# A hybrid pooling and SSD decoder layer: D times x moved from ScalarE into VectorE's sum, and the opening and the w_o pieces of the chunk stage reordered

## The chip, the core and the metric

The kernel runs on one core of one Trainium2 chip. A core has five engines with an instruction stream each: TensorE (PE in the profile; PEld is its loading of weights), VectorE (DVE), ScalarE (ACT), GpSimd (POOL) and SyncE (SP), which here only issues transfers. ACT issues transfers too, so each of the two has a queue of them. An engine takes its instructions in the order of its stream and stands still while the first one waits for a semaphore. SBUF holds tiles of 128 partitions, PSUM takes the results of matmuls in eight banks.

The metric is the time of one execution on the device in microseconds; less is better. The time before is 1295.18 us, the median of three runs (1295.17 to 1296.12).

## The reference

One layer of a decoder, for a prompt of 1024 positions and 8 samples of 8 positions, 1088 columns in all. A pooling branch and a state-space (SSD) branch run side by side and are merged by gates:

```python
shift, scale, gate = jnp.split(jax.nn.silu(c) @ w_ada + b_ada, 3, axis=-1)
h = rmsnorm(x, norm_g) * (1 + scale[:, None]) + shift[:, None]
u_pool, z_pool, z_ssm, xbc, dt_raw, g_raw = jnp.split(h @ w_in, SPLITS, axis=-1)
p, pool_new = pool_mix(u_pool, pool_buf, pos0, pool_w, pool_scale)
p = (p * jax.nn.silu(z_pool)) @ w_pool_out
xbc_c, conv_new = causal_conv(xbc, conv_buf, conv_w, conv_b)
...
y, ssm_new = ssd(xs, dt, A, Bm, Cm, ssm_state)
y = (y + d_skip[:, None] * xs).reshape(b, L, D_INNER)
y = rmsnorm(y * jax.nn.silu(z_ssm), ssm_norm_g)
s = y @ w_ssm_out
m = sigmoid(g_raw)[..., :D_MODEL] * p + sigmoid(g_raw)[..., D_MODEL:] * s
x = x + gate[:, None] * (m @ w_o)
```

The SSD goes over the prompt in chunks of 128 positions. Within one, with a lower triangular decay:

```python
decay = jnp.exp(jnp.where(mask, acs[:, :, None] - acs[:, None, :], -jnp.inf))
att = jnp.einsum('bign,bjgn->bijg', Cq, Bq)[..., None] * decay * dq[:, None]
y = jnp.einsum('bijge,bjgep->bigep', att, xq)
y = y + jnp.einsum('bign,bige,bgepn->bigep', Cq, jnp.exp(acs), h)
h = h * jnp.exp(last)[..., None, None] + jnp.einsum('bjgn,bjge,bjgep->bgepn', Bq, w_in, xq)
```

`d_skip` is the D of the title: after the SSD, D times x is added to y, a factor per head. All is in float32; the large products are made of three matmuls each on values split into a rounded high part and a low rest.

## The kernel before

**Order of the work.** The kernel is one straight program. The order in which instructions are written is not the order in which they are issued: a scheduler goes over the whole program with a model of the chip and places each instruction when the model says that its inputs and buffers are ready, so work may be issued long before its written place. Three things hold it. `in_line(engines)` chains the instructions that were written in a stretch, on the engines named, in their written order (PE through the whole chunk stage). `behind(engine)` keeps what a block writes on that engine behind the last instruction that had been written on it. And tiles have a number of buffers: a new tile of a tag waits until the oldest buffer's last reader has finished, and a pool that is opened where another was closed waits for what used that memory.

**The stages.** From 0 to about 818 us: the conditioning, h, the input projection, the convolution, the pooling, and the samples' SSD. The finished pieces go to scratch in DRAM: `xbc_d` (x, B and C after the convolution), `z_d`, `acs_d` (summed decays), `gp_d`, `gs_d` (gates). From about 818 to 1117 us the chunk stage, which the change edits. After it come the last products of w_ssm_out, the output products with w_o, and the final norm.

**The chunk stage** has 32 chunks, 4 groups g of 8 heads by 8 chunks c (i = 8g + c), and beside them the products of P (pooling) and S (SSD output), in pieces of one block of 352 or 384 columns, 12 matmuls each. `products(t)` draws about 2.56 pieces a chunk. P's pieces end in a product on DVE (line 1721), the S pieces of the first group in a copy on ACT (line 1739), those of later groups in a sum on DVE (line 1742); either frees one of the three PSUM buffers `mm`. The four buffers `ps` serve the chunks.

A chunk is a generator (`chunk`, line 1488) with these steps:

1. Loads of `xb` (line 1491; x, B and C of the chunk, 384 KB, three buffers) and `dec` (line 1187, in `decays`, 512 KB, three buffers), both on SP.
2. ACT makes `cE` (line 1498, but for c = 0); POOL masks `dec` (`far`, line 1192); ACT turns it into 8 exponentials (`exps`, line 1201).
3. The row: load of `sz`; PE turns x, 4 transposes (line 1506), and B (1508), and multiplies B by C (1509) into `pbc`; ACT copies `bt` (1511) and C (1513); DVE makes `xd` (1517), `xw` (1519, one buffer) and multiplies `dec` (1520) and `cE` (1522) by parts of `pbc`. ACT makes `xD`, D times x, in four copies with a scale (line 1525).
4. PE multiplies the new state (1530) and the output `pi` (`inner`, 1213 and 1216). The state is carried on (1534 on ACT, or 1536 on POOL and 1538 on DVE). DVE adds `pi` and `xD` (line 1542). `finish` multiplies by z on DVE (1468), squares on ACT (1469), adds squares on POOL (1470 to 1476), and splits into high `yh` on ACT (1478) and low `yl` on POOL (1479).
5. For c = 7 the last state is transposed and stored through a tile of the tag `xD` (lines 1549 to 1551).

The loop (line 1798) interleaves them: chunk i+1's row, P and S pieces, chunk i's step 4, chunk i+3's loads, chunk i+2's step 2, more pieces. Ahead of it, step 1 and 2 of chunk 0 are written into the stage before (`samples_beside`), and four pieces of P before chunk 0's row.

**The w_o pieces** (`wo_splits`, line 1766): w_o is read in 16 pieces of 128 x 512, each rounded on ACT into `ph` (line 1777, one buffer), stored from ACT (1778), subtracted on POOL (1779) and the rest stored from SP (1773). The raw pieces `pw` have two buffers. The loop calls it twice a chunk from the 14th on.

**The states' update of the samples** (line 1329) is not touched: four times on DVE, `h0` times a per-partition factor plus PSUM, 128 columns each.

## Time and profile before

| | |
|---|---|
| median of the runs | 1295.18 us |
| the profiled execution's own time | 1297.28 us |
| its span | 1295.4 us |
| its mean granted TensorE clock | 0.996 |
| PE busy in its span | 1258.9 us |
| bytes moved | 251.68 MB |

The span runs from the first to the last instruction of the profiled execution. Durations in the profile come from that one execution; times in it are counted from the span's start. A group's row reads: line, engine, operation, tile written <- tiles read, shapes, count | busy time, mean ns of one | idle time of the engine just before them and what ended it. A row of waits reads: who <- whom, us in total, times, the longest. A row of a timeline reads: start, duration, engine, line, operation, tiles, count, and in brackets the idle time before it and what ended that. A row of one line's instructions gives the least, median and greatest duration in ns and the first and last start. DMAs in a timeline stand where they are issued; PEq, ACTq, SPq are the sequencers.

### The profile page before, as it was taken

Reading aid. Unit: us, or ns where it says so; the run is one execution under the profiler, and the core shown is the slowest. Engines: PE = TensorE matmul, PEld = TensorE weight load, DVE = VectorE, ACT = ScalarE, POOL = GpSimd, SP = SyncE. Lnnn points to the kernel's source line nnn. Section 1 sums busy time; section 2 is a strip of 40 time slices with the busy share of each in tenths; the row PEclk is TensorE's granted clock in tenths of the full one; section 3 lists DMA queues with packets and bytes.
Section 4 is the critical chain, followed back from the end, with each engine's and each line's share of the span. In section 5 each row is a group of like instructions: output and inputs, shape, how many; then the busy total and the mean of one; then the engine's idle time right before and its main releaser. Section 6 shows DMA issues by size and latency. Waiting matters only on the chain.

```text
span 1295.4 us, 26382 instructions
## 1 busy us (share of the span) xinstructions
PE 1258.9 (97%) x9739; PEld 1170.7 (90%) x9739; DVE 893.3 (69%) x1512; ACT 699.5 (54%) x1658; POOL 671.9 (52%) x563
## 2 busy tenths in 40 slices
PE   7999999999999999999999999999998999999998
PEld 6779999989999999999999999888897889999786
DVE  4686678966979688676766675577665877476433
ACT  4665347365656555555666543687886776201111
POOL 1007668677868777564445444266675656214000
PEclk9999999999999999999999999999999999999999
DMA  9736355465456544444566574999887665475631
GB/s 330 242 115 223 113 163 164 147 203 177 136 161 212 157 144 149 151 146 135 169 182 192 154 207 159 336 362 382 296 270 249 200 210 171 160 262 161 227 105 50
DMA packets 233793, 251.68 MB, mean 194 GB/s; under 512 B 31265, under 2 KB 177905, under 8 KB 233658
## 3 DMA queue, kind: packets, MB, share of 16 engines
q1 hardware_dynamic: 161568, 171.60, 41.6%
q10 hardware_dynamic: 72098, 78.41, 17.6%
q8 instruction: 77, 1.26, 0.4%
q14 instruction: 50, 0.41, 0.1%
HBM read 167.06 MB, written 83.01 MB: 193 GB/s over the span
## 4 chain that ended last, share of the span: by engine, by line
PE 73%; issue 8%; DMA 6%; POOL 4%; ACT 4%; DVE 4%; ACTq 0%; SPq 0%; POOLq 0%; DVEq 0%
PE mm L608 7%; PE ps L608 7%; PE ps L609 7%; PE ps L610 7%; PE mm L610 6%; PE mm L609 6%; PE mm L359 4%; PE mm L360 4%; PE mm L361 4%; PE ps L1213 2%; PE ps L1997 2%; PE ps L1995 2%; PE ps L1996 2%; PE pc L1530 2%; PE ps L1216 2%
## 5 line engine op out<-in xcount | busy, mean ns | idle before, releaser
L168 POOL TENSOR_TENSOR wlo<-rawA,whi 128x512 fp32r<-128x512 f32 x120 | 180.0, 1505 | 176.8 <-ACT whi L165 100.3
L168 POOL TENSOR_TENSOR wlo<-raw,whi 128x512 fp32r<-128x512 f32 x92 | 147.2, 1607 | 123.2 <-ACT whi L165 109.3
L359 PE MATMUL mm<-Y,whi 128*128 128x352 f32 (+1 forms) x480 | 164.2, 342 | 2.0 <-ACT G L1739 1.4
L360 PE MATMUL mm<-Y,whi 128*128 128x352 f32 (+1 forms) x480 | 158.1, 329 | 1.0 <-DVE Y L1566 1.0
L361 PE MATMUL mm<-Y,wlo 128*128 128x352 f32 (+1 forms) x480 | 157.5, 328 | 0.0
L608 PE MATMUL mm<-Y,whi 128*128 128x272 f32 x496 | 146.5, 295 | 0.7 <-DVE GA L624 0.5
L610 PE MATMUL mm<-Y,wlo 128*128 128x272 f32 x496 | 144.2, 291 | 2.9 <-POOL wlo L168 2.4
L608 PE MATMUL ps<-Y,whi 128*128 128x272 f32 x496 | 143.4, 289 | 2.3 <-ACT o L808 2.2
L609 PE MATMUL ps<-Y,whi 128*128 128x272 f32 x496 | 143.0, 288 | 0.0
L609 PE MATMUL mm<-Y,whi 128*128 128x272 f32 x496 | 142.6, 288 | 0.0
L610 PE MATMUL ps<-Y,wlo 128*128 128x272 f32 x496 | 142.6, 287 | 0.0
L1056 DVE SCALAR_TENSOR_TENSOR GA<-GA,cvT,GA 128x1112 f32<-128x1112 f32 x72 | 128.5, 1787 | 1.6 <-ACT GA L1053 1.5
L165 ACT ACTIVATE whi<-rawA 128x512 fp32r<-128x512 f32 x125 | 78.3, 627 | 88.8 <-PE ps L609 44.9
L165 ACT ACTIVATE whi<-raw 128x512 fp32r<-128x512 f32 x96 | 58.9, 627 | 105.7 <-DVE raw L554 51.3
L359 PEld LDWEIGHTS mm<-Y,whi 128*128 128x128 f32 x480 | 90.8, 189 | 8.8 <-issue 4.6
L610 PEld LDWEIGHTS mm<-Y,wlo 128*128 128x128 f32 x496 | 93.4, 188 | 4.7 <-POOL wlo L168 3.5
L608 PEld LDWEIGHTS mm<-Y,whi 128*128 128x128 f32 x496 | 93.3, 188 | 3.4 <-ACT whi L165 0.7
L608 PEld LDWEIGHTS ps<-Y,whi 128*128 128x128 f32 x496 | 93.3, 188 | 2.9 <-ACT o L808 2.4
L609 PEld LDWEIGHTS mm<-Y,whi 128*128 128x128 f32 x496 | 93.4, 188 | 0.9
L610 PEld LDWEIGHTS ps<-Y,wlo 128*128 128x128 f32 x496 | 93.4, 188 | 0.0
L609 PEld LDWEIGHTS ps<-Y,whi 128*128 128x128 f32 x496 | 93.3, 188 | 0.0
L360 PEld LDWEIGHTS mm<-Y,whi 128*128 128x128 f32 x480 | 90.8, 189 | 1.7 <-DVE Y L1566 1.6
(450 smaller groups left out, 3801.1 us busy)
## 6 DMA issues: line engine op xcount, KB each, us to landing
rawA<-in_w_in SPq DMA_DIRECT2D x46, 512.0 KB
dec<-acs_d SPq DMA_DIRECT2D x32, 512.0 KB
xbc<-GA ACTq DMA_DIRECT2D x24, 512.0 KB
xb<-xbc SPq DMA_DIRECT2D x32, 384.0 KB
rawA<-in_w_in SPq DMA_DIRECT2D x32, 256.0 KB
pw<-in_w_ssm_out ACTq DMA_DIRECT2D x32, 256.0 KB
ws<-ph ACTq DMA_DIRECT2D x32, 256.0 KB
ws<-pw SPq DMA_DIRECT2D x32, 256.0 KB
```

The costliest lines, as they stand in the source:

```text
L165: ins = act(hi[:, :, :ncols], raw[:, :, :ncols], AF.Copy)
L168: (eng or nc.gpsimd).tensor_tensor(lo[:, :, :ncols], raw[:, :, :ncols], hi[:, :, :ncols].bitcast(F32), ALU.subtract)
L359: mm(ps[:, :n], a, rh[k][:, o:o + n], start=(k == 0), stop=False)
L360: mm(ps[:, :n], a, rl[k][:, o:o + n], start=False, stop=False)
L361: mm(ps[:, :n], b, rh[k][:, o:o + n], start=False, stop=(k == nk - 1))
L608: mm(p, hi, ah, start=(k == 0), stop=False)
L609: mm(p, hi, al, start=False, stop=False)
L610: mm(p, lo, ah, start=False, stop=(k == 3))
L1056: V.scalar_tensor_tensor(d[:, :n], rp[:, k:k + n], cvT[:, 24 * k + mc:24 * k + mc + 1], d[:, :n], ALU.mult, ALU.add)
L1213: mm(o[hh], xd[:S, 2 * q + hh, :], dec[:S, 2 * q + hh], start=True, stop=state is None)
L1216: mm(o[hh], state[:, h * 64:h * 64 + 64], cE[:, h], start=False, stop=True)
L1530: mm(pu, bt, xw.rearrange("p h d -> p (h d)"), start=True, stop=True)
```

## The change

D times x is no longer copied by ScalarE: the sum of `pi` and `xD` becomes four `scalar_tensor_tensor` on VectorE, each 128 columns of x times the factor plus `pi`. The tag `xD` goes; the last states get a tile `fo` of their own, one buffer in the pool `ck`. In `finish` the copy to `yh` and the subtraction to `yl` come ahead of the squares. For the first chunk the row is written ahead of `far` and `exps`, and ahead of all pieces of P; `far` and `exps` of the first chunk leave the stage before; the opening's instructions are chained on PE, ACT and DVE instead of on PE, and the `behind` blocks of the first chunks go. In `wo_splits` a piece is rounded one step later than before, its rest is stored in the step after, and what the calls in the loop write is kept behind ACT, SP and POOL.

```diff
-    CKL = ("sz", "xD", "v")
+    CKL = ("sz", "v")
...
         V.tensor_tensor(v, v, sz, ALU.mult)
+        yhc = yh[g][:, :, o:o + S]
+        act(yhc, v, AF.Copy)
         act(sz, v, AF.Square)
+        nc.gpsimd.tensor_tensor(yl[g][:, :, o:o + S], v, yhc.bitcast(F32), ALU.subtract)
         nc.gpsimd.tensor_tensor(sz[:, 0:2], sz[:, 0:2], sz[:, 2:4], ALU.add)
...
-        yhc = yh[g][:, :, o:o + S]
-        act(yhc, v, AF.Copy)
-        nc.gpsimd.tensor_tensor(yl[g][:, :, o:o + S], v, yhc.bitcast(F32), ALU.subtract)
...
-        far(dec, c)
-        exps(dec, g, c)
-        yield
+        if g > 0 or c > 0:
+            far(dec, c)
+            exps(dec, g, c)
+            yield
         sz = ckt([P, 4, P], "sz", 3)
...
+        if g == c == 0:
+            yield
+            far(dec, c)
+            exps(dec, g, c)
         V.tensor_tensor(dec, dec, pbc[:, P:2 * P].unsqueeze(1).to_broadcast([P, 8, P]), ALU.mult)
...
-        xD = ckt([P, 4, P], "xD")
-        for q in range(4):
-            act(xD[:, q], xb[:, q], AF.Copy, scale=Dv[:, 4 * g + q:4 * g + q + 1])
...
-        V.tensor_tensor(v, pi, xD, ALU.add)
+        for q in range(4):
+            V.scalar_tensor_tensor(v[:, q], xb[:, q], Dv[:, 4 * g + q:4 * g + q + 1], pi[:, q], ALU.mult, ALU.add)
         finish(g, o, P, v, sz)
...
-            fo = ckt([P, 4, P], "xD")
+            fo = ckt([P, 4, P], "fo", 1)
...
-        if due[0] == 7 * LAST - 1:
-            with behind(mybir.EngineType.Activation):
-                next(seq[0])
...
-            if n > 1:
-                load(wo_d[(n - 2) // 2][:, 1, n % 2 * 512:n % 2 * 512 + 512], raws.pop(n - 2))
             yield
-            if n < 16:
+            if 0 < n < 17:
                 hi = ck.tile([P, 512], F32R, tag="ph", name=nm("ph"), bufs=1)
-                act(hi, raws[n], AF.Copy)
...
+                act(hi, raws[n - 1], AF.Copy)
...
+                lo = raws.pop(n - 1)
             yield
+            if 0 < n < 17:
+                load(wo_d[(n - 1) // 2][:, 1, (n - 1) % 2 * 512:(n - 1) % 2 * 512 + 512], lo)
...
-    in_line((mybir.EngineType.PE,), True)
-    with behind(mybir.EngineType.Activation):
-        next(seq[1])
-    for _ in range(FRONT):
+    first_engines = (mybir.EngineType.PE, mybir.EngineType.Activation, mybir.EngineType.DVE)
+    in_line(first_engines, True)
+    next(seq[0])
+    for _ in range(FRONT - 1):
         next(pc_)
     next(seq[0])
+    next(seq[1])
+    next(pc_)
+    in_line(first_engines)
     for i in range(len(seq)):
         if i > 12:
-            next(wos, None)
+            with behind(mybir.EngineType.Activation), behind(mybir.EngineType.SP), behind(mybir.EngineType.Pool):
+                next(wos, None)
         if i + 1 < len(seq):
-            with behind(mybir.EngineType.DVE, 1 - i) if i < 2 else ExitStack():
-                next(seq[i + 1])
+            next(seq[i + 1])
         products(i + 0.4)
...
         if i + 2 < len(seq):
-            with behind(mybir.EngineType.Activation) if i == 0 else ExitStack():
-                next(seq[i + 2])
+            next(seq[i + 2])
         products(i + 1.0)
```

The second call of `wo_splits` in the loop gets the same three `behind`.

More of the change, by code (lines that the diff above doesn't have):

```diff
@@ L1771, in wo_splits @@
                 load(raws[n], w_o[0, n // 2 * P:n // 2 * P + P, n % 2 * 512:n % 2 * 512 + 512])
-            if n > 1:
-                load(wo_d[(n - 2) // 2][:, 1, n % 2 * 512:n % 2 * 512 + 512], raws.pop(n - 2))
             yield
-            if n < 16:
+            if 0 < n < 17:
                 hi = ck.tile([P, 512], F32R, tag="ph", name=nm("ph"), bufs=1)
-                act(hi, raws[n], AF.Copy)
-                store_(wo_d[n // 2][:, 0, n % 2 * 512:n % 2 * 512 + 512], hi.bitcast(F32))
-                nc.gpsimd.tensor_tensor(raws[n].bitcast(F32R), raws[n], hi.bitcast(F32), ALU.subtract)
+                act(hi, raws[n - 1], AF.Copy)
+                store_(wo_d[(n - 1) // 2][:, 0, (n - 1) % 2 * 512:(n - 1) % 2 * 512 + 512], hi.bitcast(F32))
+                nc.gpsimd.tensor_tensor(raws[n - 1].bitcast(F32R), raws[n - 1], hi.bitcast(F32), ALU.subtract)
+                lo = raws.pop(n - 1)
             yield
+            if 0 < n < 17:
+                load(wo_d[(n - 1) // 2][:, 1, (n - 1) % 2 * 512:(n - 1) % 2 * 512 + 512], lo)
     wos = wo_splits()
@@ L1807, in tile_pool_ssd_step @@
         if i > 12:
-            next(wos, None)
+            with behind(mybir.EngineType.Activation), behind(mybir.EngineType.SP), behind(mybir.EngineType.Pool):
+                next(wos, None)
         next(seq[i], None)
```

## The prediction

> **What bounds the kernel now.** First the page's busy shares and its chain of waits, by engine.

> ```profile
> PE 1258.9 (97%) x9739; PEld 1170.7 (90%) x9739; DVE 893.3 (69%) x1512; ACT 699.5 (54%) x1658; POOL 671.9 (52%) x563
> PE 73%; issue 8%; DMA 6%; POOL 4%; ACT 4%; DVE 4%; ACTq 0%; SPq 0%; POOLq 0%; DVEq 0%
> ```

> TensorE sets the time, and the change leaves its matmuls as they are. What can be won is the time in which PE stands still, so I next read what PE waited for from 806 us, just ahead of the chunks, to 1104 us, and the busy time by stretch.

> ```profile
> PE ps L1506 <- DVE cE L1522: 2.1, 1, 2.1
> PE ps L1508 <- DVE cE L1522: 1.7, 1, 1.7
> PE mm L359 <- ACT G L1739: 1.4, 1, 1.4
> PE pc L1530 <- ACT bt L1511: 1.3, 1, 1.3
> PE mm L360 <- DVE Y L1566: 1.0, 1, 1.0
> PE ps L1213 <- DVE dec L1520: 0.4, 1, 0.4
> ```

> ```profile
> 842.00:971.00 129.00, 129.00 (x1052) 114.61 (x1051) 92.48 (x119) 105.73 (x293) 90.11 (x99) 1.00 0.97 327
> 971.00:1004.00 33.00, 27.81 (x212) 24.18 (x211) 17.62 (x25) 20.89 (x58) 18.53 (x21) 1.00 0.78 251
> 1004.00:1104.00 100.00, 100.00 (x819) 88.52 (x817) 78.48 (x114) 73.45 (x208) 61.15 (x77) 1.00 0.61 188
> ```

> Six waits, 7.9 us, are all of it; apart from them PE is busy 100% of the chunk stage (the columns are stretch, its length, then PE, PEld, DVE, ACT, POOL busy). The table is a little short: a matmul's record runs some 0.15 us into the next one's.

> ```profile
> 818.85 0.33 PE L361 MATMUL mm<-Y,wlo 128*128 128x384 f32 x1
> 819.02 0.34 PE L359 MATMUL mm<-Y,whi 128*128 128x384 f32 x1
> 820.40 0.45 PE L360 MATMUL mm<-Y,whi 128*128 128x384 f32 x1 [1.04 <-DVE Y L1566]
> ```

> From start to start these are 0.17 apart, then 1.38: the wait is worth 1.21, not 1.04. With 0.14 more for each of the six, PE loses 7.9 + 0.8 = 8.7 us. That is the ceiling of the gain.

> Three of the waits, 2.7 listed (3.1 from start to start), lie at the opening; three, 5.2 listed (5.6), between 977 and 1003 us. Their causes on ACT and DVE:

> ```profile
> 833.29 0.69 DVE L1519 TENSOR_TENSOR xw<-ps,wdT 128x512 f32<-128x512 f32 x1 [3.91 <-DMA gs<-u]
> 834.49 0.25 ACT L1511 ACTIVATE bt<-ps 128x128 f32<-128x128 f32 x1
> ```

> ```profile
> 975.61 0.63 ACT L1777 ACTIVATE ph<-pw 128x512 fp32r<-128x512 f32 x1 [2.96 <-DMA pw<-in_w_o]
> 978.37 0.44 ACT L1739 ACTIVATE G<-mm 128x352 f32<-128x352 f32 x1
> 984.49 0.33 ACTq L1778 DMA_DIRECT2D wo<-ph  x1
> 991.97 0.63 ACT L1777 ACTIVATE ph<-pw 128x512 fp32r<-128x512 f32 x1 [4.82 <-DMA wo<-ph]
> 993.00 1.28 ACT L1525 ACTIVATE xD<-xb,Dv 128x128 f32<-128x128 f32 x4 [0.40 <-DMA out<-xD]
> ```

> ```profile
> 970.96 0.33 SPq L1771 DMA_DIRECT2D pw<-in_w_o  x1
> ```

> The second group is the w_o pieces' doing. ACT runs in order; at 972.65 it came to the rounding of a piece whose load had been issued at 970.96, and stood 2.96 us. Everything behind it was late: the copy L1739 that frees a PSUM buffer, and by way of L1513 the two products of DVE that free `pbc`. PE lost 1.4 + 2.1. At 987.15 ACT stood 4.82 us more for the store of the one `ph` buffer; PE lost 1.7 at 1001.

> **The change part by part.**

> *D times x.* Removed from ACT: 4 copies a chunk, and their waits; added on DVE: 4 products-and-sums of 128 columns in place of one sum of 512.

> ```profile
> L1525 ACT ACTIVATE xD<-xb,Dv 128x128 f32<-128x128 f32 x120 | 38.8, 390 | 22.1 <-DVE v L1542 17.4 <-DVE xd L1517 3.3 <-DMA out<-xD 1.4
> L1542 DVE TENSOR_TENSOR v<-ps,xD 128x512 f32<-128x512 f32 x29 | 19.9, 686 | 3.9 <-PE ps L1216 3.5 <-PE ps L1213 0.4
> 780.77 2.16 DVE L1329 SCALAR_TENSOR_TENSOR h<-h,E,ps 128x128 f32<-128x128 f32 x8 [1.38 <-PE ps L1326]
> ```

> ACT gains 38.8/120 x 4 = 1.29 us a chunk and up to 22.1 us of standing in all. The new form stands in the trace: the states' update L1329, SBUF times a per-partition scalar plus PSUM, 8 in 2.16 us, 0.27 each. Four cost 1.08 against 0.69: DVE +0.39 a chunk, 12.5 us over 32 chunks. On the path it costs nothing while DVE has room: it is busy 78.5 of the 100 us from 1004 on, so some 83 after (11.5 chunks). Without that cover it would be 12.5 us.

> Whether 0.27 holds beside a busy POOL is the open price.

> ```profile
> L1468 DVE TENSOR_TENSOR v<-v,sz x36: 425/750/1828, 841.4 to 1113.7; 128x512 f32<-128x512 f32 x32, 128x256 f32<-128x256 f32 x4
> ```

> L1468, two inputs in SBUF, runs from its least to 2.4 times its median (750 to 1828 ns); L1542, one of two in PSUM, hardly varies. Bounds 0.27 and 0.27 x 1828/750 = 0.66 for one, so +0.39 to +1.95 a chunk; I take 0.27, the same form. At the upper end DVE would be at 78.5 + 1.95 x 11.5 = 101 of 100, the bound. [...]

> *xb is held longer.* `xb` was last read by the ACT copies, early in a chunk; now the sum reads it, last. Its three buffers turn, so the load for chunk i+3 waits on SP for chunk i's sum, with all SP has behind it (decays, z, weights), and PE's transposes of chunk i+3 wait for the load.

> ```profile
> 1059.00 0.52 SPq L1491 DMA_DIRECT2D xb<-xbc  x1
> 1069.09 0.35 SPq L1187 DMA_DIRECT2D dec<-acs_d  x1
> 1076.04 0.32 SPq L459 DMA_DIRECT2D whi<-ws  x1
> ```

> ```profile
> 1070.88 0.68 DVE L1542 TENSOR_TENSOR v<-ps,xD 128x512 f32<-128x512 f32 x1
> 1081.06 0.60 PE L1506 MATMUL ps<-ident,xb 128*128 128x128 f32 x4
> ```

> The 30th load goes out at 1059.00, 22 us ahead of its transposes at 1081.06. After the change it can't go before the sum at 1070.88 has ended, at 1072.0 with 0.39 more: 9.1 us ahead. How long does a load of 384 KB take? The w_o piece above, 256 KB, took from 970.96 to 975.6, 4.6 us; by size that gives 6.9, so 4.6 to 6.9, and 2.2 to 4.5 us are left. I cost it at nothing. Without that room: behind the weight load that SP held until 1076.04 it goes out at 1076.4 and lands at 1081.0 to 1083.3, so PE waits 0 to 2.3 us.

> *Opening.* The 7 transposes and products of chunk 0 go ahead of the pooling products, which stood at 819 for DVE.

> ```profile
> 827.98 0.60 PE L1506 MATMUL ps<-ident,xb 128*128 128x128 f32 x4
> 828.75 0.60 PE L1506 MATMUL ps<-ident,xb 128*128 128x128 f32 x4
> ```

> They take 828.75 - 827.98 = 0.77 us and fill that much of the 1.21. `bt` (ACT, 834.49), `xw`, `xd` and the decay product move some 8 us ahead of PE's need, so the waits of 1.3 and 0.4 (2.0 from start to start) go. Sum 2.7. What can spoil it: ACT and DVE are now kept in written order, and `xw`, which waited until 833.29 for a store of the stage before, stands ahead of the sums that free the pooling products' PSUM (a rival below). The decays' mask and 8 exponentials of chunk 0 leave the stage before, where PE has no wait on them.

> *w_o pieces.* A piece is rounded one step later, about a chunk after its load was issued: a chunk is (1081.06 - 827.98)/29 = 8.7 us, the load 4.6. The store of `ph` took 984.49 to 991.97, 7.5 us, and the next rounding now comes 8.7 us on. Both ACT waits go, and with them the 5.6.

> ```profile
> L1771 SPq DMA_DIRECT2D pw<-in_w_o x16: 332/486/2146, 830.7 to 981.9; - x16
> L1864 SPq DMA_DIRECT2D Y<-wo x7: 320/422/517, 1135.1 to 1202.1; - x7
> SPq L1771 <- DMA wo<-pw: 12.4, 6, 5.7
> ```

> The trace has the pieces 120 us ahead of their written place (they are written into the loop from the 14th chunk on and start at 830.7, beside the 1st). Kept behind SP, ACT and POOL they now start near 950, where the DMA share is soon 0.61 instead of 0.97, and end near 1100, 35 us before the first load of the finished w_o at 1135.1. On SP a piece's load still waits for the store of the piece two before it, up to 5.7 us, with the chunk's loads behind it. It did so before without PE waiting for a chunk's load; I cost it at nothing, and let it count for the last rival. The subtractions on POOL have its idle time, 39 of 100 us from 1004 on.

> *Copy ahead of square; own buffer for last states.* Same instructions on ACT and POOL, in another order; the own buffer drops the 0.40 at 993. Both hidden by PE's 100%.

> *Sum.* 2.7 + 5.6 = 8.3 off. For new short waits I allow 0.6 (the least of the six, 0.4 + 0.14, is nearest), with bounds 0 and 2.1, the largest. Net 7.7: the span of 1295.40 becomes 1287.7. The profiled execution's own time, 1297.28, is 1.9 above its span and 2.1 above the median of 1295.18; the saving is the same for each, so the median becomes 1287.5. Own range: 1286.4 (all 8.7) to 1289.8.

> **Rivals.**

> *The pieces go on hurting.* If the wait at 975.6 comes back at another chunk, 3.8 us (1.4 + 2.1 + 0.3) stay: 1291.3. For: one `ph` buffer, two `pw`, a 7.5 us store against 8.7. Against: ACT has 1.29 us a chunk more.

> *The opening is spoilt.* If `xw` still waits until 833.3, the pooling sums behind it on DVE start near 834, and PE, which has three PSUM buffers for them and comes to the fourth block near 826 (four were done by 827.98), stands about 8 us; the cluster's gain is used up: 1295. For: 3.91 <- DMA gs<-u. Against: the buffers lie elsewhere, since one is added, and that ACT may store sooner; no row shows it.

> *xb comes late: slower.* The load sits behind another wait of SP's at half the 29 chunks that reload, 1.15 us (the middle of 0 to 2.3) each: 14.5 x 1.15 = 17 lost, 8 won, 1304. It decides from 0.38 us a chunk (11 us over 29), where the time passes 1297.8. For:

> ```profile
> SPq L459 <- PE mm L361: 29.8, 12, 6.7
> ```

> SP stands 2.5 us on average in 12 such waits, 6.7 at most. Against: the decays, three buffers too, are loaded behind the same chunk's matmuls already, and PE waits for none. DVE as the bound is the same sign, and needs the upper price.

> **How the numbers follow.** Forecast 60%, pieces 12%, opening 10%, `xb` 18%. A measurement of this kernel can't tell less than about 0.2% (2.6 us) from no change: faster means under 1292.6, so 72%; within 10%; slower 18%. The range runs from below the ceiling's 1286.4 up to 1296.5, past the spoilt opening, and leaves the slower case out.

> **What would show it.** Right: PE's waits from 806 to 1104 sum to 1 us or less; the pooling products' wait is near 0.4; no ACT wait of over 1 us on L1777's line; the four sums take 1.1 us together; the transposes never wait for `xb`. Wrong: PE's transposes (L1506) wait for DMA xb or SP's L1491 stands for DVE longer than 4 us; DVE over 95% busy in the chunks; PE standing near 826 for the pooling sums.

## The result, and the profile after

The changed kernel takes 1299.75 us (median of 19 runs, 1296.54 to 1302.65); the kernel before took 1295.17 us in as many runs on the same chips. The ratio is 1.0030, 95% interval 1.0018 to 1.0042: slower by 0.3%, about 4.6 us. The forecast was 1287.5, its range ran from just under 1286.4 to 1296.5; both missed, on the slower side. The profiled execution took 1301.79 us, its span 1300.1, at a mean granted TensorE clock of 0.992 (0.996 before).

First the page's busy shares, then the view of TensorE's waits over the same stretch as before, 806 to 1104 us (total us, times, longest).

```profile
PE 1263.0 (97%) x9739; PEld 1173.4 (90%) x9739; DVE 901.5 (69%) x1608; ACT 662.4 (51%) x1528; POOL 668.3 (51%) x563
```

```profile
PE ps L1507 <- DMA xb<-xbc: 6.7, 5, 2.2
PE ps L1509 <- DVE cE L1527: 1.8, 1, 1.8
PE ps L1216 <- POOL sq_acc L1479: 0.4, 1, 0.4
PE mm L360 <- DVE Y L1569: 0.3, 1, 0.3
```

The six waits of before are gone, all but 0.3 us of the opening's, as forecast. In their place stand five waits for xb and one for VectorE's `cE`: 9.2 us listed where 7.9 were. (Lines have moved: x is turned at 1507, B at 1509, the products that free `pbc` stand at 1525 and 1527, the four sums at 1545, the w_o pieces at 1771 to 1781.)

Part of the loss is not in that table. The view by stretch, here in steps of 3.41 us, has the granted clock in the third column from the end.

```profile
869.86:873.27 3.41, 1.17 (x8) 0.91 (x7) 0.89 (x2) 0.76 (x3) 0.27 (x1) 1.00 0.93 283
873.27:876.69 3.42, 1.61 (x8) 1.24 (x9) 3.19 (x4) 1.89 (x5) 2.61 (x5) 0.50 0.54 177
876.69:880.10 3.41, 3.41 (x13) 3.41 (x13) 3.03 (x8) 2.79 (x9) 1.29 (x2) 0.50 0.93 294
880.10:883.51 3.41, 3.41 (x39) 2.48 (x38) 2.82 (x4) 0.76 (x3) 2.06 (x3) 1.00 0.83 225
...
1101.96:1105.38 3.42, 3.42 (x14) 3.42 (x13) 3.42 (x8) 1.45 (x3) 2.79 (x3) 0.50 0.88 240
```

PE waits at 870.6, and from 873.27 on it runs at half speed for 6.83 us: "busy" for the whole of 876.69 to 880.10, but with its matmuls of 352 columns 0.29 us from start to start, where they are 0.16 apart at full clock. (The 39 of the next stretch are mostly shorter ones.) The same follows the wait of 1099.5, for 3.42 us. In the chunk stage the kernel before shows no half clock at all. 10.25 us at half speed are up to 5.1 us lost. That holds for the profiled execution, whose clock, 0.992, is among the lowest of the nineteen. Their mean is 0.9942, and 0.9956 in the 122 executions of the kernel before that were timed beside the experiments; the difference of 0.0014 comes to 1.8 us an execution.

What made PE stand at 870 is seen on VectorE and on SyncE's queue (start, us, instruction, idle before it and what ended it).

```profile
863.95 0.68 DVE L1518 TENSOR_TENSOR xd<-ps,dtT 128x512 f32<-128x512 f32 x1
872.05 0.43 DVE L1468 TENSOR_TENSOR v<-v,sz 128x256 f32<-128x256 f32 x1 [7.42 <-DMA v<-ys]
...
873.50 1.22 DVE L1525 TENSOR_TENSOR dec<-dec,ps 128x1024 f32<-128x1024 f32 x1 [0.56 <-ACT ps L1514]
874.64 1.21 DVE L1527 TENSOR_TENSOR cE<-cE,ps 128x1024 f32<-128x1024 f32 x1
```

```profile
863.59 0.53 SPq L1485 DMA_DIRECT2D v<-ys  x1
864.21 0.58 SPq L1491 DMA_DIRECT2D xb<-xbc  x1
```

```profile
870.62 0.32 PE L361 MATMUL mm<-Y,wlo 128*128 128x352 f32 x1
873.18 1.02 PE L1507 MATMUL ps<-ident,xb 128*128 128x128 f32 x4 [2.24 <-DMA xb<-xbc]
876.00 0.45 PE L1509 MATMUL ps<-ident,xb 128*128 128x128 f32 x1 [1.81 <-DVE cE L1527]
```

Once in each group, behind the fourth chunk, the samples' rows are finished too (`sample_end`: loads of their gate and of `ys_d`, and line 1468 on 64 columns of each quarter). In the changed kernel their product is issued on VectorE ahead of the next chunk's `dec` and `cE` products; its operand was asked for at 863.59 and is there at 872.0, so VectorE stands 7.42 us with everything behind it. In the kernel before the same product stood behind those two and, in this group, waited for nothing:

```profile
872.62 1.22 DVE L1522 TENSOR_TENSOR cE<-cE,ps 128x1024 f32<-128x1024 f32 x1
873.75 0.94 DVE L1468 TENSOR_TENSOR v<-v,sz 128x256 f32<-128x256 f32 x1
```

The change leaves that product and its loads as written. The scheduler, which places each instruction by its own model, drew a new order.

Start to start, PE's waits over 0.25 us in the chunk stage sum to 11.87 us against 8.74: +3.1. With up to 5.1 at half clock, of which some 1.7 is in those waits already, that is 6.5; by the records of PE, from the last matmul of line 610 to the first that adds up the squares, the stage took 323.0 us against 316.6, +6.4. The stages ahead of it took 1.4 less, those after it 0.3 less. With the clock's mean share, 1.8, in place of this execution's, waits and clock come near the 4.6 of the medians; the waits, 3.1, are those of one execution each.

### The profile page after: what moved, and what is told of

Same layout as the page of the kernel before. It is cut to its first block, busy times and chain, and to the rows that moved or that the text cites. A ratio compares the mean times of both kernels' runs of the same rounds, so it can differ in the third digit from the quotient of the medians.

```text
span 1300.1 us, 26323 instructions
## 1 busy us (share of the span) xinstructions
PE 1263.0 (97%) x9739; PEld 1173.4 (90%) x9739; DVE 901.5 (69%) x1608; ACT 662.4 (51%) x1528; POOL 668.3 (51%) x563
## 3 DMA queue, kind: packets, MB, share of 16 engines
q8 instruction: 77, 1.26, 0.4%
## 4 chain that ended last, share of the span: by engine, by line
PE 62%; issue 7%; DMA 6%; POOL 4%; DVE 3%; ACT 2%; ACTq 0%; SPq 0%; POOLq 0%; DVEq 0%
PE ps L608 6%; PE ps L609 6%; PE ps L610 6%; PE mm L608 6%; PE mm L610 6%; PE mm L609 5%; PE mm L359 4%; PE mm L360 3%; PE mm L361 3%; PE ps L1213 2%; PE ps L1999 2%; PE ps L2001 2%; PE ps L2000 2%; PE pc L1532 2%; POOL wlo L168 2%
## 5 line engine op out<-in xcount | busy, mean ns | idle before, releaser
L359 PE MATMUL mm<-Y,whi 128*128 128x352 f32 (+1 forms) x480 | 165.7, 345 | 0.6 <-DVE G L1902 0.5
L360 PE MATMUL mm<-Y,whi 128*128 128x352 f32 (+1 forms) x480 | 159.4, 332 | 0.3 <-DVE Y L1569 0.3
L361 PE MATMUL mm<-Y,wlo 128*128 128x352 f32 (+1 forms) x480 | 158.7, 331 | 0.0
L359 PEld LDWEIGHTS mm<-Y,whi 128*128 128x128 f32 x480 | 91.9, 191 | 7.1 <-issue 4.8
L608 PEld LDWEIGHTS mm<-Y,whi 128*128 128x128 f32 x496 | 93.4, 188 | 3.3 <-ACT whi L165 0.7
L1201 ACT ACTIVATE dec<-dec,acT 128x128 f32<-128x128 f32 (+1 forms) x288 | 86.5, 383 | 18.4 <-POOL dec L1192 18.0
L609 PEld LDWEIGHTS mm<-Y,whi 128*128 128x128 f32 x496 | 93.7, 189 | 0.9
```

The source lines that it names most:

```text
L359: mm(ps[:, :n], a, rh[k][:, o:o + n], start=(k == 0), stop=False)
L360: mm(ps[:, :n], a, rl[k][:, o:o + n], start=False, stop=False)
L361: mm(ps[:, :n], b, rh[k][:, o:o + n], start=False, stop=(k == nk - 1))
L608: mm(p, hi, ah, start=(k == 0), stop=False)
L609: mm(p, hi, al, start=False, stop=False)
L1201: act(dec[:, h], dec[:, h], AF.Exp, bias=acT[:S, c, 8 * g + h:8 * g + h + 1], scale=-1.0)
```

## The experiments

Theories, by the letters that the expectations use: **H**, the sums hold `xb` and its refill is late; **D**, VectorE's added time; **Q**, the pieces' loads and stores stand on SyncE; **C**, stretches at half clock by chance; **F**, the last states' store holds a buffer that others need; **S**, the sample rows' product stands in front on VectorE. Each run is compared with the kernel before on the same chips; the kernel after stands at 1.0030.

| run | edit | median us | ratio | 95% interval |
|---|---|---|---|---|
| e8 | before + D times x | 1295.16 | 0.9996 | 0.9982 to 1.0010 |
| e12 | before + order in finish | 1294.73 | 0.9998 | 0.9985 to 1.0011 |
| e11 | before + opening | 1298.45 | 1.0026 | 1.0013 to 1.0038 |
| e10 | before + w_o pieces | 1310.77 | 1.0123 | 1.0102 to 1.0145 |
| e1 | after, less D times x | 1315.95 | 1.0157 | 1.0141 to 1.0174 |
| e2 | after, less w_o pieces | 1297.36 | 1.0016 | 1.0005 to 1.0027 |
| e3 | after, less opening | 1300.75 | 1.0042 | 1.0028 to 1.0057 |
| e4 | after, 4 xb, states share xd | 1302.03 | 1.0050 | 1.0032 to 1.0068 |
| e5 | after, 4 xb, states in place | 1301.35 | 1.0042 | 1.0026 to 1.0059 |
| e6 | e1, states in place | 1312.05 | 1.0118 | 1.0093 to 1.0143 |
| e7 | after, sample rows' own buffers | 1303.67 | 1.0057 | 1.0038 to 1.0075 |
| e9 | after, 3 raw piece buffers | 1300.73 | 1.0041 | 1.0025 to 1.0057 |
| f1 | after, sample rows' product later | 1295.76 | 1.0005 | 0.9991 to 1.0020 |
| f2 | after, pieces behind ACT alone | 1298.79 | 1.0029 | 1.0012 to 1.0045 |
| f3 | f1 and f2 | 1293.55 | 0.9982 | 0.9966 to 0.9998 |
| f4 | after, pieces behind no engine | 1297.01 | 1.0018 | 1.0005 to 1.0031 |
| g1 | f3, 4 xb, states in place | 1296.48 | 1.0005 | 0.9991 to 1.0018 |
| g2 | f1, 4 xb, states in place | 1295.16 | 0.9998 | 0.9985 to 1.0011 |

**Less D times x (e1).** ScalarE's copies and the shared tile `xD` come back, all else stays.

```diff
-        for q in range(4):
-            V.scalar_tensor_tensor(v[:, q], xb[:, q], Dv[...], pi[:, q], ALU.mult, ALU.add)
+        V.tensor_tensor(v, pi, xD, ALU.add)
...
-            fo = ckt([P, 4, P], "fo", 1)
+            fo = ckt([P, 4, P], "xD")
```

> The kernel after with D times x copied by ScalarE again and added by one VectorE sum; the turned opening, the later w_o pieces and the new order in finish stay. Theory H (the four sums hold xb to the end of its chunk, so its refill is issued late and the transposes wait for it): the 6.7 us of TensorE waits for xb in the chunk stage fall below 1 us, and the time comes to 1288 to 1291 us, 0.4% below before, since the opening and the w_o pieces keep their gains. Theory D (the 0.39 us more per chunk on VectorE make it late): the same time, so this run does not part D from H. Theory Q (the w_o pieces' low-half stores, which now stand on SyncE's queue until VectorE or GpSimd is done, hold up the xb loads behind them): waits for xb of some 5 us stay, 1295 to 1299 us. Theory C (the records differ by TensorE stretches at half clock that come by chance): no cause in the stage, the time stays within 0.1% of the kernel after.

1315.95 us: no theory foresaw it. The moved D times x is what makes the rest bearable, not what spoils it. Of ScalarE's waits from 816 to 1130 us:

```profile
ACT xD L1530 <- DMA out<-xD: 12.2, 3, 6.7
```

The last states' store (`out<-xD`) holds one of the two `xD` buffers, and ScalarE stands up to 6.7 us at the next D times x. In the kernel before, the same wait came to 1.4 us in all.

**Less the w_o pieces (e2), less the opening (e3).** Each of the two parts in its old form within the whole change.

> The kernel after with the w_o pieces in their old order and place (split in the step that loads them). H: the waits for xb stay at 5 to 7 us, and the w_o pieces' waits of before (4.1 to 5.6 us around 977 to 1001) come back in part, as ScalarE has 1.29 us less per chunk: 1299 to 1304 us. Q: the waits for xb after 975 us (4.8 of the 6.7 us) go: 1295 to 1298 us. C: as the kernel after, within 0.1%, whatever the waits.

1.0016; the waits for xb fell to 0.5 us, but one of 6.8 us came at 836, since ScalarE stood 6.6 us for the first piece's load, followed by 10.2 us at half clock.

> The kernel after with the old opening of the chunk stage (pooling products first, chunk 0's decays before its transposes). If the opening's gain is real and its own: the waits of 1.2, 1.4 and 0.4 us at 819 to 835 us come back, 2.7 us slower than the kernel after, 1302 us. If the opening only shifts the wait to the next chunk's rows (the first waits for xb at 870 us come because the chunks start earlier): the waits for xb before 880 us go, and the time is that of the kernel after within 0.1%.

1.0042. The opening's waits are back (1.2, 0.8 and 0.3 us from start to start), but the time is not told apart from the whole change's. The difference is 0.12%, uncertain by some 0.2, so the forecast's 2.7 us (0.21%) is neither shown nor excluded.

**xb late (e4).** A fourth buffer, with the last states' tile shared with `xd` for the room.

```diff
-        xb = ckt([P, 6, P], "xb", 3)
+        xb = ckt([P, 6, P], "xb", 4)
```

> The kernel after with four xb buffers in place of three, the last states' buffer shared with xd for the room. The refill of an xb buffer then has one chunk more, some 9 us. H: the waits for xb fall below 0.5 us with VectorE's four sums kept as they are, and the time comes to 1288 to 1291 us. D: VectorE's added 0.39 us per chunk remain, so does the time, 1298 to 1300 us. Q: a load that is stuck on SyncE for 5 us no longer matters either, so 1288 to 1291 us as H; the run without the moved w_o pieces parts those two. C: the time stays with the kernel after's.

The waits for xb are gone, the time isn't: 1.0050. PE's two largest waits, and the row of VectorE's that stands behind them:

```profile
PE ps L1509 <- DVE cE L1527: 9.7, 3, 5.5
PE ps L1509 <- DVE xw L1520: 2.6, 2, 2.3
```

```profile
DVE xd L1518 <- DMA out<-xd: 13.8, 3, 8.8
```

The sharing put VectorE in ScalarE's place of e1: it stood up to 8.8 us for the last states' store.

**The same without that store (e5); e1 without it (e6).** The last states are written back into their own tile.

```diff
-            fo = ckt([P, 4, P], "fo", 1)
+            fo = hn.rearrange("p (q n) -> p q n", n=P)
```

> The kernel after with four xb buffers, and the last states written back in place into their own tile hn, so that their store holds no buffer that another step needs (in e4 VectorE stood three times, up to 8.8 us, behind that store). Theory H (the sums hold xb, and its refill is late): with neither the short refill nor the shared buffer, TensorE waits for xb and the half-clock stretches behind them go, 1288 to 1291 us. Theory S (VectorE's order puts the sample rows' product, whose operand lands 7 us late, ahead of the next chunk's products): the wait at 870 to 876 us comes back as a wait for VectorE, 1294 to 1300 us. Theory D (VectorE's added work): 1298 to 1302 us.

1.0042, level with after. No wait for xb is left; 4.1 us for `cE`, 4.0 once at 1052 us put down to a weight load, 0.7 and less stand in their place. A short refill of xb is not, by itself, what costs the time.

> The run e1 (D times x on ScalarE, the rest as after) with the last states in place in hn. Theory F (e1 lost its time because the last states' store held a buffer of xD, for which ScalarE stood 6.7 us, and VectorE and TensorE behind it): the TensorE waits of 6.5 us at 922 us goes, and the one of 6.2 us at 1036 us stays only if the sample rows' load causes it; with the half-clock stretches gone too, 1290 to 1300 us. If the copy on ScalarE itself is too much after the turned opening and the later w_o pieces: 1310 to 1316 us as e1.

1.0118 against e1's 1.0157, 0.39% or about 5 us: the shared buffer was a quarter of e1's loss. Three causes of VectorE's standing stay, by its waits:

```profile
DVE v L1468 <- DMA v<-ys: 14.9, 3, 8.1
...
DVE v L1468 <- DMA sz<-z: 7.6, 1, 7.6
DVE xw L1520 <- DMA gs<-u: 6.9, 1, 6.9
```

Two are the sample rows; the third is the opening's rival, below.

**Sample rows loaded earlier (e7).** Own tiles, loads two chunks sooner.

> The kernel after with buffers of their own for the sample rows' gate and inner product, loaded two chunks earlier. Theory S: VectorE no longer stands for these rows (17.2 us in four waits in the kernel after), the TensorE waits of 2.4 and 2.1 us at 870 to 876 us and the 6.8 us at half clock behind them go, and so does the one of 2.0 us at 1099 us with its 3.4 us: 7 to 10 us less than after, 1290 to 1293 us. Theory H: the xb loads stay late whatever the sample rows do, waits for xb of 5 us or more remain, 1297 to 1301 us.

1.0057, a miss, and an instructive one: VectorE's product moved up with its loads.

```profile
835.52 0.43 DVE L1468 TENSOR_TENSOR vs<-vs,zs 128x256 f32<-128x256 f32 x1 [9.66 <-DMA vs<-ys]
```

It now stands in the first chunks and waits 9.66 us. An earlier load does not help where the scheduler brings its user forward too.

**The parts alone (e8, e10, e11, e12).** Each part on the kernel before.

> The kernel before with this part of the change alone: D times x in VectorE's sums, and the last states' buffer of its own. Opening, w_o pieces and order in finish as before. H: waits for xb of 5 to 7 us appear, the six old waits stay in part, half-clock stretches come behind the longer ones: 1299 to 1305 us. If the loss of after comes from the turned opening or the w_o pieces' place in SyncE's queue: no waits for xb, 1293 to 1296 us.

0.9996. Waits for xb: one, 2.5 us. The later two of the old w_o waits shrink, and the sums cancel: D times x is neutral alone, and neither H nor D costs what the whole change lost.

> The kernel before with the order in finish alone changed (ScalarE's copy ahead of its square, GpSimd's low half ahead of its sums). By the forecast: nothing, 1295 us. If GpSimd's sums, now 1.3 us later, hold the gate's buffer and the loads behind it on SyncE longer: 1297 to 1300 us.

0.9998, as forecast.

> The kernel before with the opening alone changed. By the forecast: 2.7 us less, 1292 to 1293 us. From e2, where the turned opening went with w_o pieces in their old place and ScalarE stood 6.6 us for the first piece's load: the same wait of 6 to 7 us and up to 10 us at half clock near 835 us, 1297 to 1304 us. From e1 and e6, where VectorE's xw stood 6.5 to 7 us for the store of gs, a TensorE wait near 823 us: the last rival but one of the forecast, 1297 to 1300 us.

1.0026: the rival "the opening is spoilt", as its text had it. VectorE and then PE:

```profile
828.82 0.69 DVE L1520 TENSOR_TENSOR xw<-ps,wdT 128x512 f32<-128x512 f32 x1 [6.86 <-DMA gs<-u]
829.43 1.41 DVE L1723 TENSOR_TENSOR R<-mm,R 128x384 f32<-128x384 f32 x3
```

```profile
825.56 0.32 PE L361 MATMUL mm<-Y,wlo 128*128 128x352 f32 x1
830.03 0.69 PE L359 MATMUL mm<-Y,whi 128*128 128x384 f32 x1 [4.15 <-DVE R L1723]
```

```profile
828.16:831.57 3.41, 1.54 (x5) 1.54 (x6) 2.75 (x5) 3.11 (x7) 1.33 (x2) 0.50 1.08 352
831.57:834.98 3.41, 3.41 (x14) 3.31 (x13) 0.95 (x2) 0.00 (x0) 0.85 (x1) 0.50 1.12 324
```

`xw` waits for the store `gs<-u`, the pooling sums stand behind it, PE stands 4.3 us and is then at half clock for 6.8. This wait of `xw` is in the profile of all six kernels that have the `xD` tiles (before, e1, e6, e10, e11, e12; 3.8 to 6.9 us) and of none of the fourteen that don't.

> The kernel before with the w_o pieces alone changed (split one step later, kept behind ScalarE, SyncE and GpSimd, low halves stored last). By the forecast: the three waits of 977 to 1003 us go, 5.6 us, 1289 to 1290 us. Theory Q: SyncE stands about 50 us for the stores, loads are late even with xb freed by ScalarE, and the gain is lost or more: 1295 to 1300 us.

1310.77 us, 15.5 over before: beyond what either side foresaw. ScalarE and VectorE at the end of the first group:

```profile
913.21 0.40 ACTq L1551 DMA_DIRECT2D out<-xD  x1
...
922.23 1.28 ACT L1525 ACTIVATE xD<-xb,Dv 128x128 f32<-128x128 f32 x4 [7.01 <-DMA out<-xD]
...
923.78 0.26 ACT L1511 ACTIVATE bt<-ps 128x128 f32<-128x128 f32 x1
924.07 0.28 ACT L1513 ACTIVATE ps<-xb 128x128 f32<-128x128 f32 x1
```

```profile
924.44 1.22 DVE L1520 TENSOR_TENSOR dec<-dec,ps 128x1024 f32<-128x1024 f32 x1 [10.72 <-issue]
```

```profile
PE ps L1508 <- DVE cE L1522: 11.5, 2, 6.8
```

The D times x of the next chunk now stands on ScalarE ahead of `bt` and C, and waits 7.01 us for the last states' store; VectorE's `dec` and `cE`, and PE behind them, stand until it has landed, and 6.8 us at half clock follow. (The row of `dec` puts its wait down to "issue", that is to nothing that the profile shows; that it waited for C's copy, L1513, is read from that copy's end at 924.35.) PE's second long wait, 4.8 us at 1007 with 3.4 at half clock behind it, has another cause: ScalarE stands 3.85 us for a piece's load, `pw<-in_w_o`, with C's copy behind the rounding. This is the kind of wait that the new place was meant to end.

**Three raw buffers (e9).**

```diff
-                raws[n] = ck.tile([P, 512], F32, tag="pw", name=nm("pw"), bufs=2)
+                raws[n] = ck.tile([P, 512], F32, tag="pw", name=nm("pw"), bufs=3)
```

> The kernel after with three buffers for the raw w_o pieces in place of two. Theory Q (in after a piece's raw load is issued right behind the low-half store that frees its buffer, so SyncE stands 50.5 us in 14 waits there, and the chunk's loads behind it are late): those waits go; the TensorE waits for xb at 1030 to 1100 us (5.4 us) and their half-clock stretch (3.4 us at half, 1.7 lost) go; 6 to 7 us less than after, 1292 to 1294 us; the waits at 870 to 876 us, ahead of the first w_o piece, stay. If the chunk's loads were late only for VectorE's sum: the SyncE waits go and the time stays at 1298 to 1301 us.

SyncE's waits at the pieces' loads, from 816 to 1130 us, in the kernel after and in e9:

```profile
SPq L1771 <- DMA wo<-pw: 50.5, 14, 5.4
```

```profile
SPq L1771 <- DMA wo<-pw: 17.8, 6, 4.9
```

33 us less of standing, and the time stays: 1.0041. Q falls as a cost of its own.

**The sample rows' product later (f1).** It is written behind the next row on VectorE; VectorE's order is otherwise nearly that of after.

```diff
-        if i % NC == 3:
-            sample_end(i // NC)
...
             next(seq[i + 1])
+        if i % NC == 4:
+            with behind(mybir.EngineType.DVE):
+                sample_end(i // NC)
         products(i + 0.4)
```

> The kernel after with the sample rows' product written behind the next chunk's row on VectorE; the rest of VectorE's order stays but for a few neighbours. Theory S (in after VectorE stands 7.4 us at these rows for their load, with the next chunk's two products behind it): the TensorE waits of 2.4 and 2.1 us at 870 to 876 us go, with the 6.8 us at half clock behind them (3.4 lost): 8 us less than after in this stage, 1291 to 1293 us, if nothing takes their place. Theory H (xb's load itself is late): a wait for xb of 2 us or more stays at 870 us, the half-clock stretch with it, 1297 to 1300 us.

1.0005: some 3 us of the 4.6 are back. The wait for `cE` and the half-clock stretch at 873 are gone; a wait for xb of 1.8 us stays at 872, and this time the clock stays full. VectorE, and PE's waits but for one of 0.3:

```profile
866.43 1.22 DVE L1525 TENSOR_TENSOR dec<-dec,ps 128x1024 f32<-128x1024 f32 x1 [0.80 <-ACT ps L1514]
...
875.52 0.43 DVE L1468 TENSOR_TENSOR v<-v,sz 128x256 f32<-128x256 f32 x1 [4.05 <-DMA sz<-z]
```

```profile
PE ps L1507 <- DMA xb<-xbc: 4.5, 3, 2.5
```

**The pieces' place (f2, f4), and both (f3).** f2: the old split, kept behind ScalarE alone. f4: the new split, kept behind nothing.

```diff
-            with behind(mybir.EngineType.Activation), behind(mybir.EngineType.SP), behind(mybir.EngineType.Pool):
+            with behind(mybir.EngineType.Activation):
                 next(wos, None)
```

> The kernel after with the w_o pieces split in the step of their load, as before, but kept behind ScalarE's written order, and only there: loads and stores are free to go early on SyncE. Theory Q: SyncE's 50 us at the pieces' loads go, no ScalarE wait for a piece's load of over 1 us, no TensorE wait from 975 us on of over 1 us; the waits at 870 to 876 us stay if they belong to the sample rows: 1293 to 1296 us. If the pieces' cost lies in ScalarE's and GpSimd's work itself, now in the second half: 1298 to 1303 us.

1.0029 (its runs spread from 1292.45, the profiled one, to 1304.78). SyncE still stands 35.1 us at the pieces' loads, so the edit did not take away what it was to take away, and the run says little about Q.

> The kernel after with the pieces' new split order but kept behind no engine: the scheduler may place them from 830 us on, as before. If the later split alone is sound and being kept behind three engines is the fault: SyncE's waits at the pieces' loads fall to some 12 us as before, no ScalarE wait for a piece of over 1 us, 1290 to 1295 us. If the later split is at fault (a raw buffer is held for a chunk more): SyncE stands 30 us or more there, 1298 to 1305 us.

1.0018; SyncE's standing falls to 7.4 us as foreseen, but ScalarE stands 6.7 us for a piece's load at 835, and PE 6.0, with 6.8 us at half clock.

> The two edits f1 and f2 together. If both causes are real and add up: TensorE's waits in the chunk stage sum to 3 us or less, no half-clock stretch there, 1286 to 1290 us, faster than before. If a wait moves elsewhere each time one is taken away, as in e5, e7 and e9: 1295 to 1300 us.

0.9982, the one version faster than before by its interval (0.02 to 0.34%); as one of nineteen intervals, and with its edge so near to nothing, that is a weak claim. The later product is worth 0.47% between f2 and f3, and 0.25% between after and f1: S holds in both pairs. PE's waits here sum to 6.7 us, more than the 3 foreseen.

**The fourth xb buffer again, where the other causes are gone (g1, g2).**

> The run f3 (sample rows' product behind the next row, w_o pieces kept behind ScalarE alone) with four xb buffers and the last states in place. f3 has TensorE waits for xb of 1.3, 2.9 and 1.8 us and 3.4 us lost to half clock. Theory H, now that the larger causes are out of the way: these go, 1286 to 1289 us. If a wait only moves to the next engine: within 2 us of f3, 1292 to 1296 us.

> The run f1 (sample rows' product behind the next row, w_o pieces as in after) with four xb buffers and the last states in place. f1 has TensorE waits for xb of 1.8 and 2.7 us and 1.7 us lost to half clock. H: they go, 1289 to 1291 us. If SyncE's 48 us at the pieces' loads then show elsewhere, at the decays or the weights that stand behind them: 1294 to 1299 us.

g1 1.0005, g2 0.9998: no gain over f3 and f1. g2's PE waits:

```profile
PE ps L1509 <- DVE cE L1527: 3.5, 1, 3.5
PE ps L1509 <- DVE xw L1520: 3.0, 2, 2.8
PE ps L1507 <- DVE cE L1527: 1.9, 1, 1.9
```

Not one wait for xb, but 8.4 us of others, where f1's waits for xb were 4.5.

## Why the prediction was wrong

**The bound, and the ceiling of 8.7 us.** Right. PE is busy 97% of the span, its matmuls are the same, and 8.0 of the 8.7 us of waits did go (0.43 and 0.30 of the opening are left).

**The step that failed is the sum's last term:** "For new short waits I allow 0.6", bounds 0 and 2.1. New waits are 11.9 - 0.7 = 11.1 us, and what they do to the clock comes on top. Of the 11.1, 7.8 are waits for `xb`, the term that was costed at nothing, and 2.1 are the one for `cE`. The allowance took the rest of the program as fixed. It isn't: a change of buffers and of a few written places redraws every engine's order, and in a stage where 8.7 us is all there is to win, the new order has waits of its own. Two hidden premises broke.

First, *an instruction that nobody touched* moved: the sample rows' product. f1 and f3 show it as the largest single cause of those tried, 0.25% and 0.47%.

Second, *a wait was priced at its own length*. PE stood 2.4 us and lost up to 3.4 more at half clock. The six waits of before, 2.25 us at most, drew none, the longest narrowly (last section), which was luck. But that profile has a stretch of 3.41 us at half clock from 56.24 us on, just behind waits of 1.26 and 0.41 us, so the price could have been read there; with it, the allowance's upper bound, one wait of 2.1, would have been near 4.

**D times x.** The price was right: four sums take 1.12 us from first start to last end (forecast 1.08), and beside a busy GpSimd (70.25 of the 100 us from 1004 on) a single one takes 336 to 352 ns:

```profile
L1545 DVE SCALAR_TENSOR_TENSOR v<-xb,Dv,ps x128: 336/343/352, 836.5 to 1118.7; 128x128 f32<-128x128 f32 x128
```

So the lower price held; in the same profile L1468, two inputs in SBUF, takes up to 2.3 times its median (1605 and 692 ns). VectorE's total rose by 8.2 us (893.3 to 901.5; the forecast had 12.5) and it is busy 74.05 of the 100 us from 1004 on: no bound. Alone the part changes nothing (e8).

```profile
1004.00:1104.00 100.00, 95.17 (x763) 84.06 (x758) 74.05 (x132) 60.12 (x154) 70.25 (x84) 0.99 0.85 262
```

**xb, "costed at nothing".** Wrong on PE's table, 6.7 us in five waits, and mis-sized: the load was put at 4.6 to 6.9 us from one of 256 KB; the one issued at 864.21 let PE go at 873.18, 9.0 us on, with the DMA engines at 0.93 in the last 3.4 of them. It had gone out only 6.7 us before PE came to it (870.94), where the forecast counted on 9.1. The slower rival had the right place and sign but not the price (17 us). And a fourth buffer, which takes these waits away, gives no time back in four tries (e4, e5, g1, g2). Waits for VectorE's products, and once for a weight load, stand in their place; from this, and not from a run of its own, I take it that these are late by about as much, and that xb is the last to come only by a little.

**The opening, 2.7.** It held inside the whole change: PE's 3.1 became 0.73, and VectorE's `xw` waited for no store. Alone the rival came instead (e11). What tells them apart is whether the `xD` tiles exist; that another buffer then lies where `gs` was stored from is argued from this, and not shown. Even where it held, e3 can't tell the gain from nothing.

**The w_o pieces, 5.6.** The three waits went, but with the sums they also go, or shrink, where the pieces are left as they were (in e2 none is over 0.7 us from 970 on; e8 keeps 2.8 us): ScalarE's free time seems to do most of it. The new place itself was the worst part alone (e10, +15.5 us): in its trace by a store that held a shared buffer, and by a piece's load. No run had e10 with a buffer of its own. "No ScalarE wait over 1 us" at the pieces was wrong:

```profile
ACT ph L1775 <- DMA wo<-ph: 9.0, 2, 5.1
```

Two of sixteen roundings come sooner than the `ph` store lands, though none of PE's listed waits is put down to them. SyncE's standing behind the stores, costed at nothing, grew from 12.4 to 50.5 us and by e9 does cost nothing that can be measured.

**The order in finish, the own buffer: nothing.** The first right (e12). The second wrong once the pieces or the opening have moved: giving the last states a place of their own was worth 0.39%, about 5 us, between e1 and e6.

**The parts don't add.** Alone they come to -0.04, -0.02, +0.26 and +1.23%; together to +0.30%. What stays open is how much each new order is chance: the medians of the fourteen kernels with the sums lie between 1293.55 and 1303.67 us, and after's 1299.75 is one of these draws.

## What to carry to other kernels

Where a scheduler orders the work and the bound engine is busy 97%, a change that frees 8 us has to be set against what a redrawn order costs, and that is of the same size: ask which instructions on the in-order engines wait for a transfer, and whether they can land in front of the critical ones, touched or not. Price a wait of the matrix engine by the window that it falls in as well as by its length: here each of the 25 windows of 3.41 us with under 1.5 us of work was followed by half clock for at least the next 3.41. A tile shared by a slow store and a frequent step is a wait kept in store (7.01 us in e10); and taking away the last of several near-equal delays uncovers the next (g2: none of f1's 4.5 us of waits for xb, 8.4 us of others).

## What the runs showed of the hardware

A wait of TensorE often cost its clock too: 34 of the 74 below were followed by half clock. Over the twenty profiles of this study I took each wait of PE of more than 1 us in the chunk stage, from start to start, and looked whether a stretch at half clock began before 4 us after its end:

| wait of PE | number | followed by half clock |
|---|---|---|
| 1.0 to 1.6 us | 20 | 0 |
| 1.6 to 2.3 us | 22 | 8 |
| 2.3 to 3.4 us | 18 | 12 |
| 3.6 to 7.0 us | 14 | 14 |

Two of the stretches stand behind two waits each. The stretches are 3.41, 6.83 or 10.24 us long, so by an estimate from these lengths a wait of 2.5 us costs 2.5, or half a stretch of 3.41 or 6.83 more: 4.2 or 5.9.

| PE busy in a window of 3.413 us | windows | followed by half clock |
|---|---|---|
| under 1.5 us | 25 | 25 |
| 1.5 to 1.8 us | 18 | 7 |
| over 1.8 us | 1734 | 0 |

The longest wait of the kernel before left 1.52 us of work in its window, and the clock stayed. The one of 1099.5 in the kernel after left 1.53, and the clock was halved. Before, then after:

```profile
981.25:984.67 3.42, 1.52 (x12) 1.54 (x13) 3.39 (x5) 3.18 (x10) 1.76 (x4) 1.00 0.73 219
984.67:988.08 3.41, 3.41 (x31) 2.65 (x31) 1.60 (x3) 2.45 (x7) 3.41 (x4) 1.00 0.59 195
```

```profile
1098.55:1101.96 3.41, 1.53 (x11) 1.27 (x10) 1.80 (x3) 3.01 (x11) 2.57 (x5) 1.00 0.82 240
1101.96:1105.38 3.42, 3.42 (x14) 3.42 (x13) 3.42 (x8) 1.45 (x3) 2.79 (x3) 0.50 0.88 240
```

So theory C holds in part: a wait near 2 us is split over two windows or not, as the grid happens to lie, and 8 of the 22 of 1.6 to 2.3 us were followed by half clock. f2's executions show the spread, with a granted clock of 0.999 in the fastest (1292.45 us) and 0.992 in the slowest (1304.78).
